# Column sums of the norms nearer to the products, squares on VectorE alone, six first tiles ahead of the second norm, and another order of the seven products

## The chip, the cores and the metric

The kernel runs on one core of one Trainium2 chip. The metric is the device time of one launch in microseconds (us); of several runs the median is taken. The engines are TensorE (PE in the profile, with its weight loads as PEld), VectorE (DVE), ScalarE (ACT), GpSimd (POOL) and SyncE (SP, which here issues the DMA transfers).

## The reference, cut to what matters

Two layers of a decoder with 1024 tokens and 1024 channels, in float32:

```
u = RMSNorm(h);  [rq|rk|rv|rg|dq|dk|dv] = u @ W_in        # 1024 x 3072
ret = silu(rg) * RMSNorm(retention(rq, rk, rv))            # 4 heads
dif = RMSNorm(differential_attention(dq, dk, dv))          # 4 heads
h = h + concat(ret, dif) @ W_out
u = RMSNorm(h)
h = h + (silu(u @ W_gate) * (u @ W_up)) @ W_down           # hidden width 2816
```

and a last RMSNorm. The change touches the norms and the feed-forward.

## The kernel before, in words

Channels lie on the partitions and tokens along the free axis, so `h` is eight tiles of 128x1024. A float32 factor is split in two parts, `hi` (a cast by ScalarE) and `lo` (the rest, a subtraction by VectorE or GpSimd), and each product takes three matmuls: hi by hi, hi by lo, lo by hi (`product`, lines 244 to 246; `mm3`, lines 268 to 270).

A norm works on one half of the tokens (512). `squares` lets ScalarE square the eight tiles of `h` and adds the squares up in one tile `acc`; VectorE does the adds, but those of k = 2 and 4 go to GpSimd. `rsqrt_rows` lets TensorE sum the columns of `acc` (line 378) into a few PSUM columns, a short chain of VectorE and ScalarE makes the inverse roots of them (lines 383 to 390), and after `gap` more units of TensorE's other work four transposes (line 394) spread the result over a bank. `yield lag` before it sets how many units of other work stand between the last square and the column sums; a unit is one matmul of 512 columns. The norm's generators are woven into the products of the output projection (`two_halves`) or of the feed-forward.

The feed-forward treats the tokens as two halves and the channels as two halves, and computes each 2x2 block product with seven products instead of eight. The right factors `b[0]` to `b[6]` come from the normed `h`: b[0] and b[1] need the first token half only (`seven_first`), the others the second half too (`seven_second`). Each of the 22 hidden tiles (`gate_up`; two weight tiles, one for gate and one for up) has seven products of 12 matmuls, numbered q = 0 to 6, into three PSUM banks `x`, `y` and `z`. Some banks are read between two products that add into them: after q = 2 ScalarE copies `x` (`u2`), after q = 3 ScalarE copies `z` (`z1`, line 951), and `c22` (line 963) is VectorE's read of `x` on the way. The order before is x y x z x z x. `first` (line 956) reads `y`, `second` (line 968) `z`, and `end` (line 973) `x`.

The left factors of a tile come from its two raw weight tiles, loaded by SP. `factors` plans their steps: `load`, `sums` (lines 903 to 905) and `last` (line 908) on VectorE, and five to seven `split`s. A split of product n is queued `LEAD` = 4 products ahead of it.

Since the second token half is normed only when TensorE is already in the feed-forward, q = 0 and 1 of the first `NPRE` = 5 tiles go ahead. Their `x` banks are kept until q = 2; the five `g0` results lie in `kb` and `acc` buffers. `seven_second` gives its steps to `Line.later`, which places them after a product with a given number. ScalarE, VectorE, GpSimd and SP have a written order in the feed-forward: each engine works its instructions off in the order of the code, and those that wait hold up those behind them. TensorE has a written order in the whole kernel.

In `down_fast` the same seven products run for two output tiles in turn (e = 0, 1), and each result is added to `h` (`add_h`, line 863). Its right factors (`right_factors`) come back from DRAM.

Of the kernel before, what the change touches and what calls it, by code (L numbers as in the profile page):

```python
# [27 lines left out]
NPRE = 5  # L28
# [3 lines left out]
TAGS7 = ["u", "u", "ka", "v", "sp", "u", "u"]  # L32
# [69 lines left out]
def shape_tables():  # L102
# [10 lines left out]
    kd = np.repeat(np.exp((P - 1 - c)[:, None] * lg[None, :]), 64, axis=1)  # L113
# [31 lines left out]
class Trunk:  # L145
# [29 lines left out]
    def consts(self):  # L175
# [5 lines left out]
        self.tabs = self.const("c_tabs", [P, 1026])  # L181
# [216 lines left out]
    def squares(self, h, sl, alone, pool, first=False):  # L398
        nc = self.nc
        tmp = (lambda: self.big("kb")[:, 0:512]) if first else self.tmp  # L400
        n = sl.stop - sl.start
        parts, acc = [], None
        for k in range(KT):
            s = (tmp() if k else self.t("acc", 1, [P, 512]))[:, :n]
            with nullcontext() if first else self.tc.high_priority():
                nc.scalar.activation(s, h[k][:, sl], AF.Square)
                if k >= KT - alone:
                    parts.append(s)
                elif acc is None:
                    acc = s  # L410
                    parts.append(s)
                else:
                    eng = nc.gpsimd if pool and k in (2, 4) else nc.vector
                    eng.tensor_tensor(out=acc, in0=acc, in1=s, op=ALU.add)
        return parts

    def norm_half(self, h, hf, gcol, us, pool=True, lag=14, first=False, keep=False):
        nc = self.nc
        sl = slice(hf * HT, hf * HT + HT)
        parts = self.squares(h, sl, 0, pool, first)  # L420
        yield lag
        y = yield from self.rsqrt_rows(parts, D)
# [14 lines left out]
    def seven_first(self, h, gcol, b, keep):  # L437

        nc = self.nc
        parts = self.squares(h, slice(0, HT), 0, True)  # L440
        yield 32
        y = yield from self.rsqrt_rows(parts, D)
# [6 lines left out]
    def seven_second(self, h, gcol, b, keep, line):  # L449
# [4 lines left out]
        parts = self.squares(h, sl, 0, True)  # L454
        yield 16
        y = yield from self.rsqrt_rows(parts, D, gap=9)
        own = self.t("u", 4, [P, KT, HT])
        b += [self.views(tag) for tag in TAGS7[2:4]]
# [3 lines left out]
        t2 = []  # L462
# [4 lines left out]

        def low(src, dst):
            v(out=dst[1], in0=src, in1=dst[0].bitcast(F32), op=ALU.subtract)

        def steps():
            b22 = self.views(TAGS7[5])
            for i in range(4):
                norm(t22[i], 4 + i)
                self.part(t22[i], b22[i], nc.gpsimd)
            yield
            for i in range(4):
                norm(t12[i], i)
            yield
            two = [self.big("sp") for _ in range(2)]  # L480
            t2.extend(two[i // 2][:, c[i % 2]] for i in range(4))
            for j in range(2):
                for i in (2 * j, 2 * j + 1):
                    v(out=b11[i], in0=t12[i], in1=b11[i], op=ALU.subtract)
                    v(out=t2[i], in0=t22[i], in1=b11[i], op=ALU.subtract)
                    nc.scalar.copy(b[2][i][0], t2[i])
                yield
            for i in range(4):
                low(t2[i], b[2][i])
                nc.scalar.copy(b[3][i][0], b11[i])  # L490
            yield
            for i in range(4):
                low(b11[i], b[3][i])
            yield
            for i in range(4):
                v(out=b21[i], in0=b21[i], in1=t2[i], op=ALU.subtract)
            yield
            b.append(self.views(TAGS7[4]))
            for i in range(4):
                v(out=b11[i], in0=t22[i], in1=t12[i], op=ALU.subtract)  # L500
                nc.scalar.copy(b[4][i][0], b11[i])
            yield
            b.append(b22)
            b.append(self.views(TAGS7[6]))
            for i in range(4):
                low(b11[i], b[4][i])
                nc.scalar.copy(b[6][i][0], b21[i])
            yield
            for i in range(4):
                low(b21[i], b[6][i])  # L510
            yield
        go = steps()
        for q in range(10):
            line.later(line.n + q, lambda: next(go))
# [259 lines left out]
    def ret_scores(self, x, n):  # L774
# [17 lines left out]
        if n < 7:  # L792
# [3 lines left out]
            nc.vector.tensor_tensor(out=kd, in0=tps[:, 0:256], in1=self.tabs[:, 768:1024], op=ALU.mult)  # L796
# [16 lines left out]
    def retention(self, l, x, mix):  # L813
# [3 lines left out]
        st = self.t("acc", 1, [P, 512])  # L817
# [5 lines left out]
        for n in range(8):  # L823
# [13 lines left out]
            if n < 7:  # L837
# [4 lines left out]
                for p in range(2):  # L842
                    for j in range(2):
# [3 lines left out]
                        nc.vector.scalar_tensor_tensor(out=sv, in0=sv, scalar=self.tabs[r, 1024 + p:1025 + p], in1=kv,  # L847
# [39 lines left out]
    def factors(self, line, at, pos, early=0, tags=("wr", "wr"), mixed=False):  # L887
# [8 lines left out]
        def split(n, i, k):  # L896
            src = s3[0] if i is None else r[i][:, c[k]]
            line.w[n] = self.wsplit(src, self.nc.vector if mixed and n % 3 == 0 else None)
# [21 lines left out]
        else:  # L920
            put(pos[2] - 4 - early, load, 0)
            put(pos[2] - 3 - early, load, 1)
            put(pos[2] - 1 - early, sums)
            put(pos[2] - 1 - early, last)
# [7 lines left out]
    def gate_up(self, line, at, b, pre, st, room, done, early=0):  # L932
# [4 lines left out]
        self.factors(line, at, {j: n0 + i for i, j in enumerate([range(7), range(2), range(2, 7)][pre])}, early)  # L937

        def go(name, tag, q):
            n = len(line.products)  # L940

            def run():
                if tag:
                    st[name] = self.bank(tag)
# [314 lines left out]
```

## Time and profile before

| | |
|---|---|
| median of 3 runs | 2340.5 us (2339.1 to 2342.1) |
| profiled execution | 2341.5 us, of which the span from first to last instruction is 2339.8 |
| TensorE busy | 2274.7 us, 97% of the span |
| VectorE, ScalarE, GpSimd busy | 1390.7 (59%), 1011.3 (43%), 850.9 (36%) us |
| DMA | 215.66 MB, mean 92 GB/s |
| granted TensorE clock | 0.988 of full speed |

The feed-forward of the first layer begins at 507.6 us of the span with the first product of tile 0. In a row of the profile `ps_mm<-u,w` means an output in a PSUM bank of tag mm made from tiles of tags u and w; numbers of buffers are left out. Times of single instructions are from the profiled execution.

### The profile page before, as it was taken

To read this page: it belongs to the slowest core of one execution; us is meant where nothing else is said; L and a number is where in the kernel's file an instruction comes from. 1 tells how busy PE (TensorE), PEld (TensorE's weight loads), DVE (VectorE), ACT (ScalarE), POOL (GpSimd) and SP (SyncE) were. 2 spreads that over 40 slices of the span, in tenths; PEclk is the share of its full clock that TensorE was granted. 3 is DMA by queue.
4 is the path that set the end of the run, shared out by engine and by line. 5 is a ranking of instruction groups with operands and counts; after the bars stand their busy time and mean duration, and the time that the engine had idled before them with its cause. 6 is when DMAs were issued, how large, how long until landed. Compare 5 with 4: busy or idle time off the path is not lost. (4 is left out here: it accounts for less than half of the span.)

```text
span 2339.8 us, 30724 instructions
## 1 busy us (share of the span) xinstructions
PE 2274.7 (97%) x11328; PEld 1906.9 (82%) x11328; DVE 1390.7 (59%) x2512; ACT 1011.3 (43%) x1905; POOL 850.9 (36%) x672
## 2 busy tenths in 40 slices
PE   7999999997999999999999999999889999999998
PEld 5888898876888888888888888988768888888887
DVE  7777603968543433896557774058874444449855
ACT  5666623434333333543246665244443333345332
POOL 4111212144545455335231112212544545544351
PEclk8999999999999999999999999999999999999999
DMA  4312121101332322753232122111123232345522
GB/s 159 81 46 64 46 91 45 55 28 56 125 126 77 126 86 92 242 164 115 73 90 55 49 70 81 56 36 54 46 94 128 77 126 77 104 145 184 185 63 73
DMA packets 73926, 215.66 MB, mean 92 GB/s; under 512 B 7984, under 2 KB 10032, under 8 KB 73776
## 3 DMA queue, kind: packets, MB, share of 16 engines
q1 hardware_dynamic: 73776, 213.70, 28.5%
q8 instruction: 89, 1.46, 0.3%
q14 instruction: 61, 0.50, 0.1%
HBM read 161.24 MB, written 44.04 MB: 88 GB/s over the span
## 5 line engine op out<-in xcount | busy, mean ns | idle before, releaser
L221 POOL TENSOR_TENSOR w<-wr,w 128x512 fp32r<-128x512 f32 x302 | 430.3, 1437 | 497.9 <-ACT w L220 466.3
L261 POOL TENSOR_TENSOR w<-wr,w 128x512 fp32r<-128x512 f32 x140 | 186.6, 1339 | 576.4 <-ACT w L260 547.5
L268 PE MATMUL ps_mm<-u,w 128*128 128x512 f32 (+1 forms) x735 | 296.6, 404 | 0.0
L270 PE MATMUL ps_mm<-u,w 128*128 128x512 f32 (+1 forms) x735 | 288.0, 392 | 0.0
L269 PE MATMUL ps_mm<-u,w 128*128 128x512 f32 (+1 forms) x735 | 287.8, 392 | 0.0
L220 ACT CAST w<-wr 128x512 fp32r<-128x512 f32 x320 | 193.2, 619 | 154.3 <-DVE wr L905 74.7
L244 PE MATMUL ps_mm<-u,w 128*128 128x512 f32 x448 | 175.6, 392 | 5.6 <-DVE t L963 5.6
L246 PE MATMUL ps_mm<-u,w 128*128 128x512 f32 x448 | 174.8, 390 | 0.0
L245 PE MATMUL ps_mm<-u,w 128*128 128x512 f32 x448 | 174.8, 390 | 0.0
L270 PEld LDWEIGHTS ps_mm<-u,w 128*128 128x128 f32 x735 | 138.4, 188 | 30.4
L951 ACT COPY t<-ps_mm 128x512 f32<-128x512 f32 x80 | 47.0, 588 | 258.6 <-PE ps_mm L246 258.6
L268 PEld LDWEIGHTS ps_mm<-u,w 128*128 128x128 f32 x735 | 138.8, 189 | 24.1
L269 PEld LDWEIGHTS ps_mm<-u,w 128*128 128x128 f32 x735 | 138.8, 189 | 23.3
L260 ACT CAST w<-wr 128x512 fp32r<-128x512 f32 x140 | 86.0, 619 | 128.8 <-PE ps_t L269 38.5
L305 PE MATMUL ps_mm<-w,u 128*128 128x256 f32 x448 | 127.1, 284 | 1.0 <-DVE u L431 1.0
L303 PE MATMUL ps_mm<-w,u 128*128 128x256 f32 x448 | 127.9, 285 | 0.0
L304 PE MATMUL ps_mm<-w,u 128*128 128x256 f32 x448 | 126.8, 283 | 0.0
L863 DVE TENSOR_TENSOR a<-a,ps_mm 128x512 f32<-128x512 f32 (+1 forms) x148 | 98.7, 667 | 45.7 <-PE ps_mm L270 27.5
L577 DVE CUSTOM_DVE_ANT_0 sp<-ps_s,wr 128x512 f32<-128x512 f32 (+2 forms) x192 | 103.2, 551 | 34.3 <-PE ps_s L575 33.1
L581 ACT ACTIVATE sp<-sp,m 128x256 f32<-128x256 f32 (+7 forms) x128 | 99.2, 775 | 53.4 <-DVE m L580 52.9
L244 PE MATMUL ps_t<-u,w 128*128 128x512 f32 x256 | 104.2, 407 | 18.5 <-DVE kb L956 18.5
L903 DVE TENSOR_TENSOR t<-wr,wr 128x512 f32<-128x512 f32 x48 | 35.4, 737 | 123.0 <-DMA wr<-wts 123.0
(364 smaller groups left out, 5959.8 us busy)
## 6 DMA issues: line engine op xcount, KB each, us to landing
wr<-wts SPq DMA_DIRECT2D x192, 512.0 KB, 3.7
mx<-s_fast SPq DMA_DIRECT2D x56, 512.0 KB, 5.2
s_fast<-mx SPq DMA_DIRECT2D x48, 512.0 KB, 4.3
kb<-ka SPq DMA_DIRECT2D x64, 128.0 KB, 2.3
s_rest<-mx SPq DMA_DIRECT2D x12, 512.0 KB, 2.9
kb<-wts SPq DMA_DIRECT2D x12, 512.0 KB, 5.4
mx<-s_rest SPq DMA_DIRECT2D x12, 512.0 KB, 3.3
a<-xT SPq DMA_DIRECT2D x16, 256.0 KB, 5.4
```

The source lines that it names most:

```text
L220: nc.scalar.copy(h, src)
L221: (eng or nc.gpsimd).tensor_tensor(out=o, in0=src, in1=h.bitcast(F32), op=ALU.subtract)
L244: mm(ps, lhsT=wh[:, c], rhs=bh, start=first and i == 0, stop=False, skip_group_check=True)
L245: mm(ps, lhsT=wh[:, c], rhs=bl, start=False, stop=False, skip_group_check=True)
L246: mm(ps, lhsT=wl[:, c], rhs=bh, start=False, stop=i == 3, skip_group_check=True)
L261: nc.gpsimd.tensor_tensor(out=o, in0=raw[:, cols], in1=h.bitcast(F32), op=ALU.subtract)
L268: mm(out, lhsT=lh, rhs=rh, start=first, stop=False)
L269: mm(out, lhsT=lh, rhs=rl, start=False, stop=False)
L270: mm(out, lhsT=ll, rhs=rh, start=False, stop=last)
L303: mm(o, lhsT=uh, rhs=wh, start=k == 0, stop=False)
L304: mm(o, lhsT=uh, rhs=wl, start=False, stop=False)
L305: mm(o, lhsT=ul, rhs=wh, start=False, stop=k == KT - 1)
```

## The change

The parts of the change, in the order of the diff:

- `NPRE` is 6 instead of 5. The sixth tile's `x` takes a bank of tag s. `hold` lets the `y` of tiles 4 and 5 share one bank, and the `z` of tiles 0 to 5 another. `acc` has two buffers instead of one; to make room, the `kd` table is stored with 4 columns instead of 256 and spread by the access pattern.
- `squares` adds on VectorE alone. The squares of `norm_half` lie in `kb` buffers.
- `lag` is 11 in all norms but the very first layer's second half and the last norm; `gap` is 9 but in the first layer's first norm and the last.
- `seven_second` gives out its steps singly, three per product and later four, in the order in which the products need their results. All splits of its factors are made by VectorE.
- `factors`: tile 0's two weight tiles are loaded ahead of the section into `sp` buffers, and its `sums` stand ahead of the norm. `own` names products whose split is on VectorE.
- The order of the seven products is x y x z z x x: those of q = 4 and 5 are swapped, with their left and right factors, in `gate_up` and in `down_fast`.

TensorE, inside a tile of the first layer's feed-forward (tile 13): ps_mm is the tile's bank `x`, ps_s its bank `z`; v, sp and u hold right factors, w the left ones. In brackets stands the engine whose semaphore is waited for. Before, the end of q = 3 and the beginning of q = 4:

```order
L246 MATMUL ps_s_6981<-v_5023,w_6914 128x512
L244 MATMUL ps_s_6981<-v_5024,w_6913 128x512
L245 MATMUL ps_s_6981<-v_5026,w_6913 128x512
L246 MATMUL ps_s_6981<-v_5024,w_6914 128x512
L244 MATMUL ps_s_6981<-v_5024,w_6913 128x512
L245 MATMUL ps_s_6981<-v_5026,w_6913 128x512
L246 MATMUL ps_s_6981<-v_5024,w_6914 128x512
L244 MATMUL ps_mm_6920<-sp_5228,w_6933 128x512 [waits Activation_49]
```

and after, at the same place:

```order
L246 MATMUL ps_s_6978<-v_5016,w_6912 128x512
L244 MATMUL ps_s_6978<-v_5017,w_6911 128x512
L245 MATMUL ps_s_6978<-v_5019,w_6911 128x512
L246 MATMUL ps_s_6978<-v_5017,w_6912 128x512
L244 MATMUL ps_s_6978<-v_5017,w_6911 128x512
L245 MATMUL ps_s_6978<-v_5019,w_6911 128x512
L246 MATMUL ps_s_6978<-v_5017,w_6912 128x512
L244 MATMUL ps_s_6978<-u_5020,w_6930 128x512 [waits Activation_49]
```

The product that follows q = 3 now adds into the same bank ps_s, and its first matmul waits for ScalarE, whose copy `z1` (`COPY t_1259_6995<-ps_s_6978`) reads that bank after q = 3. In the same way the last product, q = 6, now follows another one into ps_mm and waits for VectorE's `c22`.

VectorE in the same tile, before (t holds `u2`, `z1` and the sums' first result, wr the raw weights, mx the tile's results):

```order
L956 TENSOR_TENSOR mx_6958<-ps_t_6939,t_1250_6937 128x512
L903 TENSOR_TENSOR t_1264_7012<-wr_6956,wr_6976 128x512
L904 TENSOR_TENSOR wr_6976<-wr_6976 128x512
L905 TENSOR_TENSOR wr_6956<-wr_6976,wr_6956 128x512
L963 TENSOR_TENSOR t_1263_6998<-ps_mm_6920,t_1263_6998 128x512
L908 TENSOR_TENSOR wr_6956<-wr_6956 128x512
L968 TENSOR_TENSOR mx_6958<-ps_s_6981,t_1259_6978 128x512
L973 TENSOR_TENSOR mx_6958<-mx_6958,ps_mm_6920 128x512
```

and after:

```order
L936 TENSOR_TENSOR mx_6955<-ps_t_6936,t_1246_6934 128x512
L881 TENSOR_TENSOR t_1260_7009<-wr_6953,wr_6973 128x512
L882 TENSOR_TENSOR wr_6973<-wr_6973 128x512
L883 TENSOR_TENSOR wr_6953<-wr_6973,wr_6953 128x512
L948 TENSOR_TENSOR mx_6955<-ps_s_6978,t_1255_6975 128x512
L886 TENSOR_TENSOR wr_6953<-wr_6953 128x512
L943 TENSOR_TENSOR t_1259_6995<-ps_mm_6917,t_1259_6995 128x512
L953 TENSOR_TENSOR mx_6955<-mx_6955,ps_mm_6917 128x512
```

`c22` (line 963, now 943) and `second` (968, now 948) have changed places; ahead of `c22` stands `last` and no longer `sums`.

VectorE at the start of the first layer's feed-forward, right behind the inverse roots of the second token half, before (u is the normed half, kb the `g0` results, a the tiles of `h`):

```order
L956 TENSOR_TENSOR kb_4906<-ps_t_4976,t_901_4974 128x512
L465 SCALAR_TENSOR_TENSOR u_5018<-a_688_3898,c_gains,ps_s_5013 128x512
L465 SCALAR_TENSOR_TENSOR u_5018<-a_689_3899,c_gains,ps_s_5013 128x512
L465 SCALAR_TENSOR_TENSOR u_5018<-a_690_3900,c_gains,ps_s_5013 128x512
L465 SCALAR_TENSOR_TENSOR u_5018<-a_691_3901,c_gains,ps_s_5013 128x512
L903 TENSOR_TENSOR t_928_5074<-wr_4972,wr_5006 128x512
L904 TENSOR_TENSOR wr_5006<-wr_5006 128x512
L905 TENSOR_TENSOR wr_4972<-wr_5006,wr_4972 128x512
L908 TENSOR_TENSOR wr_4972<-wr_4972 128x512
L465 SCALAR_TENSOR_TENSOR u_5018<-a_684_3894,c_gains,ps_s_5013 128x512
```

and after:

```order
L221 TENSOR_TENSOR w_4984<-wr_4928,w_4983 128x512
L881 TENSOR_TENSOR t_905_4989<-sp_4930,sp_4932 128x512
L882 TENSOR_TENSOR sp_4932<-sp_4932 128x512
L883 TENSOR_TENSOR sp_4930<-sp_4932,sp_4930 128x512
L886 TENSOR_TENSOR sp_4930<-sp_4930 128x512
L465 SCALAR_TENSOR_TENSOR u_5011<-a_684_3894,c_gains,ps_s_5006 128x512
L465 SCALAR_TENSOR_TENSOR u_5011<-a_685_3895,c_gains,ps_s_5006 128x512
L465 SCALAR_TENSOR_TENSOR u_5011<-a_686_3896,c_gains,ps_s_5006 128x512
L936 TENSOR_TENSOR kb_4906<-ps_t_4996,t_906_4994 128x512
L221 TENSOR_TENSOR w_5048<-wr_4987,w_5047 128x512
L465 SCALAR_TENSOR_TENSOR u_5011<-a_687_3897,c_gains,ps_s_5006 128x512
```

Tile 0's `sums` have moved ahead of the norm, the read of `y` (956, now 936) comes after three steps of it, and splits of left factors (221) stand between.

The diff, cut:

```diff
-NPRE = 5
+NPRE = 6
-TAGS7 = ["u", "u", "ka", "v", "sp", "u", "u"]
+TAGS7 = ["u", "u", "ka", "v", "u", "u", "sp"]
...
-    def squares(self, h, sl, alone, pool, first=False):
+    def squares(self, h, sl, alone, kb=False, first=False):
...
-            s = (tmp() if k else self.t("acc", 1, [P, 512]))[:, :n]
+            s = (tmp() if k else self.t("acc", 2, [P, 512]))[:, :n]
...
-                    eng = nc.gpsimd if pool and k in (2, 4) else nc.vector
-                    eng.tensor_tensor(out=acc, in0=acc, in1=s, op=ALU.add)
+                    nc.vector.tensor_tensor(out=acc, in0=acc, in1=s, op=ALU.add)
...
-    def norm_half(self, h, hf, gcol, us, pool=True, lag=14, first=False, keep=False):
+    def norm_half(self, h, hf, gcol, us, lag=11, gap=9, first=False, keep=False):
...
     def seven_first(self, h, gcol, b, keep):
-        yield 32
-        y = yield from self.rsqrt_rows(parts, D)
+        yield 11
+        y = yield from self.rsqrt_rows(parts, D, gap=9)
...
     def seven_second(self, h, gcol, b, keep, line):
-        yield 16
+        yield 11
...
+        ops = [lambda i=i: norm(t12[i], i) for i in r]
+        ops += [lambda i=i: norm(t22[i], 4 + i) for i in r]
+        for i in r:
+            ops.append(lambda i=i: sub(b11[i], t12[i], b11[i]))
+            ops.append(lambda i=i: sub(t2[i], t22[i], b11[i], 2, i))
+        ops += [lambda i=i: low(t2[i], b[2][i]) for i in r]
+        ops += [lambda i=i: self.part(b11[i], b[3][i], nc.vector) for i in r]
+        ops += [lambda i=i: self.part(t22[i], b[4][i], nc.vector) for i in r]
+        ops += [lambda i=i: sub(b11[i], t22[i], t12[i]) for i in r]
+        ops += [lambda i=i: sub(b21[i], b21[i], t2[i]) for i in r]
+        for q, src in ((5, b11), (6, b21)):
+            ops.append(lambda q=q: b.append(self.views(TAGS7[q])))
+            ops += [lambda i=i, q=q, src=src: self.part(src[i], b[q][i], nc.vector) for i in r]
+        for i, op in enumerate(ops):
+            line.later(line.n + (i // 3 if i < 21 else 7 + (i - 21) // 4), op)
...
     def factors
-            put(pos[4], split, pos[4], None, 0)
-            put(pos[5], split, pos[5], 0, 1)
+            put(pos[4], split, pos[4], 0, 1)
+            put(pos[5], split, pos[5], None, 0)
...
     def gate_up
-            line.add(go("x", None, 4), c22)
-            line.add(go("z", None, 5), second)
+            line.add(go("z", None, 4), second)
+            line.add(go("x", None, 5), c22)
             line.add(go("x", None, 6), end)
...
     def feed_forward
-            st[t]["tag"] = ["mm", "mm", "mm", "o", "t"][t]
+            st[t]["tag"] = ["mm", "mm", "mm", "o", "t", "s"][t]
...
+            if t > 3:
+                st[t]["bank_y"] = hold
+            st[t]["bank_z"] = hold
...
+            kw = {"early": (-1, -1, 0), "tags": ("sp", "sp"), "own": range(2 * NPRE, 2 * NPRE + 5, 2)} if t == 0 else {}
...
     def down_fast
-                                                ("z", "s", 1, 1), ("x", None, 1, 1), ("z", None, 0, 1),
+                                                ("z", "s", 1, 1), ("z", None, 0, 1), ("x", None, 1, 1),
                                                 ("x", None, 1, 0))):
```

More of the change, by code (lines that the diff above doesn't have):

```diff
@@ L466, in norm, with sub @@
                                            in1=y, op0=ALU.mult, op1=ALU.mult)
+        def sub(out, x, z, q=None, i=0):
+            v(out=out, in0=x, in1=z, op=ALU.subtract)
+            if q is not None:
+                nc.scalar.copy(b[q][i][0], out)
         def low(src, dst):
             v(out=dst[1], in0=src, in1=dst[0].bitcast(F32), op=ALU.subtract)
[L471 to L511, printed above, removed]
@@ L512, in seven_second @@
-        go = steps()
-        for q in range(10):
-            line.later(line.n + q, lambda: next(go))
+        r = range(4)
+        ops = [lambda i=i: norm(t12[i], i) for i in r]
[5 more added lines that the diff above has]
+        ops += [lambda i=i: self.part(b11[i], b[3][i], nc.vector) for i in r]
@@ L920, in factors @@
         else:
[L921 to L924, printed above, removed]
+            n = pos[2] - LEAD
+            n0, n1, n2 = early or (n - 4, n - 3, n - 1)
+            line.later(n0, lambda: load(0))
+            line.later(n1, lambda: load(1))
+            line.later(n2, sums)
+            line.later(n2, last)
         if 2 in pos:
```

60 lines of the change are left out of this document (34 added, 26 removed).

## The prediction

> **What bounds the kernel now.** I read the page's busy shares first, then the table of stretches, then what TensorE waited for, then single rows at the places that the change touches.
>
> ```profile
> span 2339.8 us, 30724 instructions
> PE 2274.7 (97%) x11328; PEld 1906.9 (82%) x11328; DVE 1390.7 (59%) x2512; ACT 1011.3 (43%) x1905; POOL 850.9 (36%) x672
> ```
>
> TensorE is busy for 97% of the span, no other engine for more than 59%. The table of stretches shows where the rest lies. Its columns are the stretch, its length, and the busy time and instructions of PE, PEld, DVE, ACT and POOL, then the granted clock and the DMA.
>
> ```profile
> 507.00:572.00 65.00, 50.55 (x194) 39.99 (x193) 56.78 (x69) 29.60 (x54) 33.87 (x23) 0.87 0.16 49
> 572.00:970.00 398.00, 398.00 (x1749) 327.81 (x1748) 178.40 (x246) 150.09 (x268) 194.28 (x142) 1.00 0.34 115
> 1150.00:1200.00 50.00, 46.52 (x234) 39.39 (x233) 35.75 (x51) 22.38 (x42) 25.68 (x25) 0.93 0.40 137
> 1662.00:1726.00 64.00, 49.28 (x194) 38.55 (x193) 57.86 (x68) 29.45 (x53) 34.02 (x23) 0.89 0.17 50
> 1726.00:2125.00 399.00, 398.82 (x1751) 328.10 (x1750) 181.41 (x247) 149.94 (x268) 194.63 (x142) 1.00 0.35 116
> ```
>
> The two rows of 398 and 399 us are the gate and up products and the fast part of the down projection of each layer. TensorE never rests there: whatever makes it wait there adds to the time in full. The two rows of 64 and 65 us are the way into the feed-forward, where TensorE idles some 14.5 us per layer at a mean clock of 0.87 to 0.89; the row at 1150 is the norm between the layers. What TensorE waited for, over the whole span (total, times, longest), and in the stretch 1150:1200 (last row):
>
> ```profile
> PE ps_t L244 <- DVE kb L956: 18.5, 4, 5.1
> PE ps_s L378 <- DVE acc L414: 12.1, 6, 3.5
> PE ps_mm L244 <- DVE t L963: 5.6, 2, 2.8
> ...
> PE ps_s L378 <- DVE acc L414: 3.5, 1, 3.5
> ```
>
> So VectorE holds TensorE up on the way in: bank ps_t comes free only when L956 has read it, and L956 stands behind the norm's steps.
>
> **Part 1: products that write one bank twice in a row.** The diff swaps pos[4] and pos[5]. In each of the 22 tiles of a layer the second product into `z` now follows the first at once, and the last product into `x` follows the one before it at once. In between, ScalarE must copy `z` (`z1`, line 951) and VectorE must read `x` (`c22`, line 963). Before, a whole product of 12 matmuls, 2.72 us (398 us over 1749 matmuls is 0.227 each), lay over each of those reads, and the 398 us stretch shows that it hid them. Now nothing does. These rows price it: the last matmul of a `z` product and the next one, the copy behind it; the last matmul of an `x` product, the add behind it; and TensorE's restart at the one place where it already waited for that add.
>
> ```profile
> 657.15 0.39 PE L246 MATMUL ps_s<-v,w 128*128 128x512 f32 x1
> 657.38 0.40 PE L244 MATMUL ps_mm<-sp,w 128*128 128x512 f32 x1
> ...
> 657.63 0.59 ACT L951 COPY t<-ps_s 128x512 f32<-128x512 f32 x1 [1.15 <-PE ps_s L246]
> ...
> 640.81 0.39 PE L246 MATMUL ps_mm<-sp,w 128*128 128x512 f32 x1
> ...
> 641.31 0.69 DVE L963 TENSOR_TENSOR t<-ps_mm,t 128x512 f32<-128x512 f32 x1 [1.34 <-PE ps_mm L246]
> ...
> 569.02 0.68 DVE L963 TENSOR_TENSOR t<-ps_mm,t 128x512 f32<-128x512 f32 x1
> ...
> 569.75 0.50 PE L244 MATMUL ps_mm<-u,w 128*128 128x512 f32 x1 [2.80 <-DVE t L963]
> 570.09 0.39 PE L245 MATMUL ps_mm<-u,w 128*128 128x512 f32 x1
> ```
>
> A matmul follows the last after 0.23 us. The copy ends at 658.22, 1.07 after the start of the last `z` matmul. TensorE restarts 0.05 us after a reader ends (569.70 to 569.75), and its first step is 0.34 instead of 0.23. So the `z` wait costs 1.07 + 0.05 - 0.23 + 0.11 = 1.00 us. The add ends at 642.00, 1.19 after its matmul: 1.19 + 0.05 - 0.23 + 0.11 = 1.12 us. A tile pays 2.12 us, 44 tiles 93 us.
>
> The lower end: a reader that starts the instant the last matmul ends (0.39) and no slow restart, 0.39 + 0.59 - 0.23 = 0.75 and 0.39 + 0.69 - 0.23 = 0.85, so 70 us. The upper end: the adds of the trace did not all find VectorE free.
>
> ```profile
> DVE t L963 <- PE ps_mm L246: 37.5, 22, 4.2
> ```
>
> 22 adds waited for the product, of the 44 that there are; the rest stood behind other work, above all the three `sums` of the next tile. If half of the new adds came 0.9 us late, 20 us more, 113 in all. I stay with 93: in the new order `sums` stand ahead of `second`, a whole product before the add, and only the single `last` (L886) comes between. ScalarE has the same cast ahead of the copy as before.
>
> In the fast down projection the same swap leaves one product between (the two sets alternate), 2.72 us for an add of 0.69; I take 0, up to 3 us where `sums` lie ahead. What is queued behind the waiting matmuls is only TensorE's own stream; loads, casts and GpSimd's splits get more time, and nothing waits for them there.
>
> **Part 2: the way into the feed-forward.** Here VectorE sets the time. Before, its norm steps run from 520.70 to the add at 569.02; first row, the stretch; second, a stretch of it with GpSimd idle:
>
> ```profile
> 520.70:569.00 48.30, 36.68 (x141) 28.62 (x140) 47.35 (x52) 22.85 (x40) 26.21 (x16) 0.89 0.15 48
> 550.10:554.90 4.80, 4.65 (x11) 3.68 (x12) 4.80 (x9) 1.67 (x3) 0.00 (x0) 0.51 0.32 105
> ...
> 507.61 0.39 PE L244 MATMUL ps_mm<-u,w 128*128 128x512 f32 x1
> 513.93 0.34 PE L378 MATMUL ps_s<-c_ones,acc 128*128 128x1 f32 x1 [2.08 <-DVE acc L414]
> ...
> 515.80 0.16 DVE L383 TENSOR_SCALAR nx<-ps_s 128x4 f32<-128x4 f32 x1 [2.02 <-PE ps_s L378]
> ...
> 516.87 0.16 DVE L390 SCALAR_TENSOR_TENSOR ny<-nx,ny 128x4 f32<-128x4 f32 x1
> ...
> 520.70 0.75 DVE L465 SCALAR_TENSOR_TENSOR u<-a,c_gains,ps_s 128x512 f32<-128x512 f32 x1 [1.44 <-PE ps_s L394]
> ```
>
> Eight instructions start in the quiet 4.80 us, 0.60 each. 52 of them alone would be 31.2 us; the stretch took 17.1 more with 16 GpSimd instructions in it, so each of those costs VectorE 1.07 us. Before, the way in began at 507.61 (product 0) and the last product of tile 0 began at 569.75, 62.1 us later; its 14 products of 2.72 us and 1.4 us of sums and transposes are 39.5, so 22.6 us were lost.
>
> After: the same stretch, from the first L465 to the first `c22`, holds 61 VectorE instructions by the order (t22's low halves and the splits of products 6, 8, 10, 12, 14 and 16 come to VectorE) and about 7 of GpSimd: 61 x 0.60 + 7 x 1.07 = 44 us. It begins earlier. Squares no longer go through GpSimd and the column sums stand one product into the section, at 2.7 us; 9 matmuls and four transposes later it is 6.2; a split and tile 0's `sums`, now ahead of the norm, hold VectorE until about 8.3. The add then ends at 8.3 + 44 + 0.7 = 53.0 us. Without waits 16 products, 1.4 us and the 2.12 of part 1 are 47.0, so 6 us stay lost, mostly as waits for L936 of products 7 and 9 (the new number of L956) and for the last right factors. The gain is 22.6 - 6 = 16.6 us per layer, 33 in both. Ends: nothing lost, 45 us; VectorE as slow per instruction as before (61 x 0.93 = 57, lost 19), 7 us. I take 33, since the 1.07 comes from this stretch itself. Tile 0's two loads now go out before the section, into `sp`, ahead of three others in SP's queue; a load lands 3.7 us after its issue (next row), well before `sums` at 5 us and the splits that use the others, so I count 0.
>
> ```profile
> wr<-wts SPq DMA_DIRECT2D x192, 512.0 KB, 3.7
> ```
>
> **Part 3: the other norms.** Between the layers the 3.48 us wait for `acc` (L414, two of its adds on GpSimd) and the slower clock after it (granted 0.93 over 50 us) cost 3.5 us and, for some nine steps at 0.43 as in the rows below, 1.8, together 5.3. With all adds on VectorE the sum should be there on time; it is also asked for three matmuls, 0.7 us, earlier. I take a gain of 4.5, between 0 and 5.3. The first-half norms had no wait; they keep 9 or more matmuls over a chain of 1.2 us (515.80 to 517.03, L383 to L390) and cost 0, at most 1 each. The kernel's first norms keep their places in TensorE's order, the smaller `kd` table is a 128x256 operation as before, squares in `kb` use two buffers in turn: 0, plus or minus 1.
>
> **Sum.** The profiled execution took 2341.5 (span 2339.8). 2341.5 + 93 - 33 - 4.5 = 2397. It lay 1.0 above the median of the runs, 2340.5, so I predict 2396, slower by 2.4%.
>
> **The clock after a wait.** These rows show TensorE 3 us behind the idle of 2.08 at 513.93, behind one of 4.14 and behind one of 1.25:
>
> ```profile
> 517.05 0.63 PE L244 MATMUL ps_t<-u,w 128*128 128x512 f32 x1
> 517.48 0.63 PE L245 MATMUL ps_t<-u,w 128*128 128x512 f32 x1
> ...
> 540.52 0.50 PE L244 MATMUL ps_t<-u,w 128*128 128x512 f32 x1 [4.14 <-DVE kb L956]
> ...
> 541.45 0.63 PE L244 MATMUL ps_t<-u,w 128*128 128x512 f32 x1
> 541.88 0.63 PE L245 MATMUL ps_t<-u,w 128*128 128x512 f32 x1
> ...
> 130.50 0.52 PE L600 MATMUL ps_t<-c_ident,sp 128*128 128x128 f32 x3 [1.25 <-DVE sp L662]
> 130.77 0.48 PE L268 MATMUL ps_mm<-u,w 128*128 128x512 f32 x1
> 131.09 0.39 PE L269 MATMUL ps_mm<-u,w 128*128 128x512 f32 x1
> ```
>
> After the two long ones steps are 0.43, half speed; after the short one they are not. The new waits idle 0.7 to 0.9 us, so I add nothing. [...]
>
> **Rivals.**
> A. The waits are hidden after all, and the time falls: TensorE reaches the second `z` product only once the copy is done. For it: ScalarE and VectorE are less than half busy in the 398 us stretch. Against: the copy cannot start before the product ends, and no other matmul stands between. It decides at (33 + 4.5) / 88 = 0.43 us per wait; at no cost the time is 2303. Chance 0.04.
> B. Each wait, or each pair, brings the half clock, some nine steps of 0.43 instead of 0.23, 1.8 us: 44 to 88 times, 79 to 158 us, 2475 to 2554. For it: an idle of 2.08 us was enough. Against: the 1.25 above. Chance 0.06.
> C. The way in gains nothing, because VectorE, with 9 instructions more, is as late as before: 2396 + 33 = 2429. For it: VectorE was full there (56.78 of 65 us). Against: 16 GpSimd instructions become about 7. Chance 0.06.
> D. My forecast. With 80 to 110 for the waits and 50 to 25 for all gains together it is 2340.5 + 80 - 50 = 2370 to 2340.5 + 110 - 25 = 2425; the outer ends of both at once I leave out. Chance 0.80. The last 0.04 is for sums between these, around 2350.
>
> **How the numbers follow.** 2396 is D's. The range 2370 to 2425 is D's, and leaves out 0.20. A measurement of this kernel can tell about 0.2%, 4.7 us. Faster: A, 0.04. Same: 0.01, where a cheap wait just meets the gain. Slower: D, B, C and most of the rest, 0.95.
>
> **What would show it.** In the stretch of the gate and up products the waits of TensorE list L931 (the copy, on ScalarE) and L943 (the add) some 44 times each, at 0.7 to 1.0 us, with the granted clock still at 1.00, and a tile takes 21.2 us instead of 19.05. On the way in the waits for the ps_t bank shrink but stay; at 1180 there is no wait over 1 us. I am wrong if those two lines are missing or near 0.2 us, or if steps of 0.43 appear behind them.

## The result: slower by 3.1%, and the profile after

| | before | after | ratio (95% interval) |
|---|---|---|---|
| median of the runs | 2341.3 us (2339.1 to 2343.4, 4 runs) | 2414.8 us (2411.2 to 2416.4, 4 runs) | 1.0312 (1.0294 to 1.0330) |
| span of the profiled execution | 2339.8 us | 2414.6 us | |

The change costs 73.5 us; 55.5 were forecast, and the time lies in the range of 2370 to 2425. The page of the changed kernel, and its table of stretches (length, busy time and instructions of PE, PEld, DVE, ACT and POOL, then the granted clock and the DMA):

```profile
PE 2293.5 (95%) x11328; PEld 1896.0 (79%) x11328; DVE 1391.1 (58%) x2552; ACT 1008.7 (42%) x1905; POOL 784.6 (32%) x632
```

```profile
505.00:565.00 60.00, 53.39 (x223) 42.64 (x222) 52.62 (x76) 28.35 (x53) 19.75 (x12) 0.94 0.16 46
580.00:990.00 410.00, 379.52 (x1618) 300.25 (x1617) 163.97 (x227) 135.69 (x243) 172.24 (x131) 1.00 0.31 105
1190.00:1240.00 50.00, 46.31 (x245) 39.89 (x245) 34.40 (x52) 22.35 (x41) 25.39 (x23) 0.93 0.39 137
```

In the gate and up products (second row), where TensorE had been busy for all of 398 us, it now rests 30.5 us of 410, at a granted clock of 1.00. On the way in (first row) it rests 6.6 of 60 us instead of 14.5 of 65. The norm between the layers (third row) is as it was: 46.3 of 50 us busy, clock 0.93. What TensorE waited for, over the whole span (total, times, longest):

```profile
PE ps_s L244 <- ACT t L931: 35.2, 44, 2.9
PE ps_mm L244 <- DVE t L943: 31.0, 38, 1.4
PE ps_s L244 <- DVE a L841: 7.9, 6, 2.6
```

L931 (the copy of `z`) and L943 (`c22`) are there 44 and 38 times (six more `c22` waits, 5 us, stand under the banks ps_t, ps_o and ps_s, for tiles whose `x` lies there). L841 is the add of the down projection, a line that had no entry there before.

The start of each of the 210 products of a feed-forward can be read from both traces. What a stage took beyond 2.722 us for each of its products, both layers together, against the terms of the prediction:

| stage | before | after | difference | forecast |
|---|---|---|---|---|
| up to the first feed-forward | 507.6 | 505.2 | -2.4 | 0 |
| way in, to the end of tile 0 | 47.3 | 24.8 | -22.5 | -33 + 4.2 for two waits a layer |
| tiles 1 to 21 | 3.2 | 91.0 | +87.8 | +89 |
| fast down projection | 2.2 | 12.7 | +10.6 | 0 |
| between the feed-forwards | 556.3 | 556.6 | +0.3 | -4.5 |
| behind the second one | 79.9 | 81.0 | +1.1 | 0 |

The differences add up to 74.9, the spans differ by 74.8. The waits have the size that was forecast; the two gains are smaller, and the down projection is a loss that the forecast did not have.

One tile of the steady state, by the time of its instructions (start, length, engine, line; in brackets the idle before it and what ended that):

```profile
675.22 0.39 PE L246 MATMUL ps_s<-v,w 128*128 128x512 f32 x1
676.28 0.50 PE L244 MATMUL ps_s<-u,w 128*128 128x512 f32 x1 [0.68 <-ACT t L931]
676.62 0.39 PE L245 MATMUL ps_s<-u,w 128*128 128x512 f32 x1
...
681.63 0.39 PE L246 MATMUL ps_mm<-u,w 128*128 128x512 f32 x1
682.80 0.50 PE L244 MATMUL ps_mm<-sp,w 128*128 128x512 f32 x1 [0.79 <-DVE t L943]
683.14 0.39 PE L245 MATMUL ps_mm<-sp,w 128*128 128x512 f32 x1
...
675.64 0.59 ACT L931 COPY t<-ps_s 128x512 f32<-128x512 f32 x1 [1.09 <-PE ps_s L246]
...
682.06 0.69 DVE L943 TENSOR_TENSOR t<-ps_mm,t 128x512 f32<-128x512 f32 x1 [1.43 <-PE ps_mm L246]
```

Both readers had been idle before (1.09 and 1.43 us) and start 0.42 and 0.43 us after the start of the last matmul of their product. The step from 675.22 to 676.28 is 1.06 instead of 0.23, that from 681.63 to 682.80 is 1.17, and behind each one step of 0.34 follows; then TensorE is at 0.23 again. That is 0.95 + 1.05 = 2.0 us; from tile to tile it comes to 2.0 to 2.1.

### The profile page after: what moved, and what is told of

The parts are those of the page before. It is cut to its first block, busy times and chain, and to the rows that moved or that the text cites. A ratio compares the mean times of both kernels' runs of the same rounds, so it can differ in the third digit from the quotient of the medians.

```text
span 2414.6 us, 30677 instructions
## 1 busy us (share of the span) xinstructions
PE 2293.5 (95%) x11328; PEld 1896.0 (79%) x11328; DVE 1391.1 (58%) x2552; ACT 1008.7 (42%) x1905; POOL 784.6 (32%) x632
## 4 chain that ended last, share of the span: by engine, by line
PE 78%; DVE 12%; ACT 4%; issue 2%; DMA 2%; POOL 0%; DVEq 0%; SPq 0%; ACTq 0%; POOLq 0%
PE ps_mm L244 8%; PE ps_mm L246 7%; PE ps_mm L245 7%; PE ps_mm L268 6%; PE ps_mm L270 6%; PE ps_mm L269 6%; PE ps_s L244 5%; PE ps_s L246 4%; PE ps_s L245 4%; PE ps_mm L305 2%; PE ps_mm L303 2%; PE ps_mm L304 2%; PE ps_t L244 2%; PE ps_t L246 2%; PE ps_t L245 2%
## 5 line engine op out<-in xcount | busy, mean ns | idle before, releaser
L221 POOL TENSOR_TENSOR w<-wr,w 128x512 fp32r<-128x512 f32 x282 | 380.3, 1359 | 472.4 <-ACT w L220 468.4
L261 POOL TENSOR_TENSOR w<-wr,w 128x512 fp32r<-128x512 f32 x140 | 185.8, 1333 | 565.6 <-ACT w L260 539.2
L931 ACT COPY t<-ps_mm 128x512 f32<-128x512 f32 x76 | 44.7, 588 | 345.2 <-PE ps_mm L246 345.2
L244 PE MATMUL ps_mm<-u,w 128*128 128x512 f32 x432 | 168.5, 390 | 0.0
L246 PE MATMUL ps_mm<-u,w 128*128 128x512 f32 x432 | 168.4, 390 | 0.0
L245 PE MATMUL ps_mm<-u,w 128*128 128x512 f32 x432 | 168.2, 389 | 0.0
L221 POOL TENSOR_TENSOR w<-t,w 128x512 fp32r<-128x512 f32 x54 | 79.9, 1480 | 230.2 <-ACT w L220 230.2
L244 PE MATMUL ps_s<-u,w 128*128 128x512 f32 x256 | 107.9, 422 | 43.1 <-ACT t L931 35.2
L841 DVE TENSOR_TENSOR a<-a,ps_mm 128x512 f32<-128x512 f32 (+1 forms) x148 | 98.6, 667 | 48.5 <-PE ps_mm L246 35.0
```

The lines of the kernel that those rows point to most:

```text
L221: (eng or nc.gpsimd).tensor_tensor(out=o, in0=src, in1=h.bitcast(F32), op=ALU.subtract)
L244: mm(ps, lhsT=wh[:, c], rhs=bh, start=first and i == 0, stop=False, skip_group_check=True)
L245: mm(ps, lhsT=wh[:, c], rhs=bl, start=False, stop=False, skip_group_check=True)
L246: mm(ps, lhsT=wl[:, c], rhs=bh, start=False, stop=i == 3, skip_group_check=True)
L261: nc.gpsimd.tensor_tensor(out=o, in0=raw[:, cols], in1=h.bitcast(F32), op=ALU.subtract)
```

## Experiments

In these kernels a line or two were added near the top, so that the line numbers are higher by one to three: L245 is the product's first matmul, L379 the column sums, L414 the squares' add, L842 the add of the down projection. `ORD` is the old order in the new numbering.

**1. The old order back.** The version with all of it:

```diff
+ORD = (0, 1, 2, 3, 5, 4, 6)
 def gate_up
+        order = ORD if pre != 2 or at != self.ff_at else range(7)
-        self.factors(line, at, {j: n0 + i for i, j in enumerate([range(7), range(2), range(2, 7)][pre])}, **kw)
+        self.factors(line, at, {j: n0 + i for i, j in enumerate([order, order[:2], order[2:]][pre])}, **kw)
...
-            line.add(go("z", None, 4), second)
-            line.add(go("x", None, 5), c22)
+            two = {4: ("z", second), 5: ("x", c22)}
+            for q in order[4:6]:
+                line.add(go(two[q][0], None, q), two[q][1])
 def right_factors, down_fast
-        for q in range(7):
+        for p, q in enumerate(ORD):
```

> The changed kernel with the old order x y x z x z x of the seven products in the tiles 1 to 21 of each layer and in the fast down projection; tile 0 and everything else as changed. Theory (the swap costs what the trace of the changed kernel shows: 44.2 and 43.6 us in tiles 1 to 21 of the two layers, 6.5 and 4.1 us in the down projection, and the rest of the change is a gain): 2414.8 - 87.8 - 10.6 = 2316 us, below the kernel before. Rival 1 (the down projection's waits come from VectorE's splits there, not from the order): 2327 us. Rival 2 (the waits return at other places, because the six tiles ahead or the splits on VectorE cause them): above 2341 us.

> The same, but the down projection keeps the changed order (z after z, x after x). Theory: 2414.8 - 87.8 = 2327 us, with waits for L841's successor in the down projection of 6 to 10 us in all as in the changed kernel. If the order in the down projection costs nothing, this and the kernel with both undone give the same time.

Measured: 2319.7 us with both undone, ratio to the kernel before 0.9908 (0.9893 to 0.9922); 2332.2 us with the down projection left in the new order, 0.9960 (0.9945 to 0.9975). They lie 4 and 5 us above the 2316 and 2327 that were expected; no run here looks for these few us. The gate and up products of the first, a stretch of its table:

```profile
580.00:940.00 360.00, 360.00 (x1582) 296.63 (x1582) 158.43 (x213) 133.02 (x239) 179.16 (x130) 1.00 0.34 115
```

No rest is left there. So the swap is the whole of the loss: without it the change is a gain of some 20 us. The second kernel keeps this row among TensorE's waits, which the first does not have:

```profile
PE ps_s L245 <- DVE a L842: 10.2, 6, 3.0
```

Its down projections take 13.7 us beyond their products, those of the first 2.5; the medians differ by 12.5. Rival 1 falls too: VectorE has as many splits in both kernels, and only the one with the new order waits 10 us for the add.

**2. The swap alone, in the kernel before.**

```diff
+ORD = (0, 1, 2, 3, 5, 4, 6)
-        self.factors(line, at, {j: n0 + i for i, j in enumerate([range(7), range(2), range(2, 7)][pre])}, early)
+        self.factors(line, at, {j: n0 + i for i, j in enumerate([ORD, ORD[:2], ORD[2:]][pre])}, early)
-            line.add(go("x", None, 4), c22)
-            line.add(go("z", None, 5), second)
+            line.add(go("z", None, 5), second)
+            line.add(go("x", None, 4), c22)
```

> The kernel before with one edit: the products q = 4 and 5 of each hidden tile change places (x y x z z x x), in the gate and up products only. Theory (the price belongs to the order alone, 2.04 us a tile): 2341.3 + 42 x 2.04 = 2427 us, up to 4 more for the two tiles 0. Rival (the price needs the other parts of the change, such as the splits on VectorE): near 2341 us. A second rival (half of the adds stand behind the three sums of the next tile, 0.9 us late): 2447 us.

Measured: 2425.2 us, 1.0360 (1.0343 to 1.0378), 85 us more than the kernel before. Its waits (L952 is `z1`, L964 is `c22`):

```profile
PE ps_mm L245 <- DVE t L964: 33.4, 40, 1.7
PE ps_s L245 <- ACT t L952: 31.1, 44, 1.2
```

The tiles 1 to 21 of both layers take 87.1 us more than before, 2.07 a tile, and the way in 1.8 less. The price is that of the order, in either kernel: putting the order into the kernel before costs 85, taking it out of the changed kernel's gate and up products brings 83. The adds behind `sums` do not come late by the 20 us of the second rival, since in this order too `sums` stand ahead of `second`.

**3. How long a pause may be before the clock falls.**

```diff
-                nc.scalar.copy(st[to], st[name])
+                for _ in range(1 + more):
+                    nc.scalar.copy(st[to], st[name])
```

`more` is 0 but for `z1` of the tiles 7 to 18, where it is 1, 2, 3 and 4 for three tiles each.

> The changed kernel; in the tiles 7 to 18 of each layer ScalarE copies z one to four times more before the second z product may start (three tiles with each number), in the others as changed. The idle of TensorE before that product should be 0.8 us with no extra copy and then some 1.3, 1.85, 2.4 and 2.9. Theory P (a wait costs its length and one slow step): 60 extra copies x 0.53 = 32 us, 2447 us, no step of 0.43 behind any of the waits. Theory C (past an idle of about 2 us the clock halves for 1.8 us): the 12 tiles with three or four more pay 1.8 each besides, 2469 us, with steps of 0.43 behind those waits and none behind 0.8 and 1.3.

Measured: 2466.3 us (one run). In the rows L246 to L248 are a product's matmuls and L934 the copy. Waits of 1.29 us (one more copy) and of 1.91 us (two more), and the stretches behind three waits:

```profile
677.03 0.50 PE L246 MATMUL ps_s<-u,w 128*128 128x512 f32 x1 [1.29 <-ACT t L934]
677.37 0.39 PE L247 MATMUL ps_s<-u,w 128*128 128x512 f32 x1
...
742.96 0.50 PE L246 MATMUL ps_s<-u,w 128*128 128x512 f32 x1 [1.91 <-ACT t L934]
743.29 0.39 PE L247 MATMUL ps_s<-u,w 128*128 128x512 f32 x1
...
744.56 0.63 PE L246 MATMUL ps_s<-u,w 128*128 128x512 f32 x1
744.98 0.63 PE L247 MATMUL ps_s<-u,w 128*128 128x512 f32 x1
```

```profile
742.96:744.20 1.24, 1.24 (x5) 1.04 (x6) 1.14 (x2) 0.46 (x1) 0.70 (x1) 1.00 0.00 0
744.20:747.60 3.40, 3.40 (x10) 2.60 (x9) 1.39 (x2) 0.62 (x1) 1.88 (x2) 0.52 0.00 0
...
864.64:868.05 3.41, 3.40 (x15) 2.83 (x16) 0.35 (x1) 0.99 (x2) 2.54 (x2) 1.00 0.00 0
...
840.22:843.20 2.98, 2.98 (x7) 2.40 (x8) 0.41 (x1) 1.06 (x2) 2.44 (x2) 0.50 0.03 5
```

All six waits of 1.29 us are followed by steps of 0.34, then 0.23. Behind the 1.91 us the first steps are fast as well; 1.24 us later the clock is at half for 3.4 us and each step is 0.43. So it went six times out of six. Of the longer waits some did nothing: one of 2.52 us ended at 840.22 with the half clock behind it, the next of the same length at 864.64 without. Twelve of the 18 waits of 1.9 us and more cost 1.3 to 1.6 us besides their length. The time is that of theory C, but not by its rule: there it should have been the 12 with three or four copies.

**4. The same length each time.** As in the kernel of the last experiment, with `more` = 3 in the tiles 4 to 20.

> The changed kernel with three extra copies of z before the second z product in the tiles 4 to 20 of each layer: 34 waits of the same length, an idle of some 2.5 us each. In the run with one to four extra copies, waits of this length had steps of 0.43 behind them in four cases and none in two, and the places where the clock fell lay on a grid of 3.41 us. Theory G (the clock is set for each window of 3.41 us by the idle in the window before; it halves where that idle is over some 1.75 us): whether a wait costs 1.6 us more depends on where in the grid it falls; 72% of places do ((3.41 - 2.53 + 2 x 0.78) / 3.41), some 24 of 34 waits, in runs of neighbouring tiles, since a tile of 23 to 24.6 us is near seven windows: 2414.8 + 102 x 0.58 + 24 x 1.6 = 2512 us. Rival I (each wait past an idle of about 2 us brings the half clock, and the two exceptions had another cause): all 34, 2528 us. Rival N: the length of the wait alone counts from the second such wait on: 2475 us.

Measured: 2507.1 us (one run). Two neighbouring waits of the same length:

```profile
687.62 0.80 PE L246 MATMUL ps_s<-u,w 128*128 128x512 f32 x1 [2.53 <-ACT t L934]
688.22 0.63 PE L247 MATMUL ps_s<-u,w 128*128 128x512 f32 x1
...
712.14 0.50 PE L246 MATMUL ps_s<-u,w 128*128 128x512 f32 x1 [2.53 <-ACT t L934]
712.48 0.39 PE L247 MATMUL ps_s<-u,w 128*128 128x512 f32 x1
```

Of the 34 waits 20 had the half clock behind them (24 by theory G, 34 by I, none by N), 14 had not; a tile takes some 24.6 us with the half clock and 23.0 without, so that the wait moves on, and the two kinds mostly alternate. So the length of a wait alone, 2.53 us in both of these rows, did not decide here; its place did, as G says. Where the places lie is read from the granted clock of the same trace. Here are two stretches at half clock with the one between them, and then two windows of 3.41 us, each with the window that follows it (the granted clock is the third number from the end):

```profile
1858.16:1861.57 3.41, 3.41 (x9) 2.65 (x9) 0.00 (x0) 0.25 (x1) 2.38 (x2) 0.50 0.98 326
1861.57:1923.01 61.44, 51.41 (x219) 40.48 (x219) 19.34 (x29) 22.97 (x41) 21.61 (x17) 1.00 0.22 75
1923.01:1926.42 3.41, 3.41 (x9) 2.67 (x8) 0.00 (x0) 0.66 (x2) 2.52 (x2) 0.50 0.00 0
...
803.44:806.85 3.41, 1.44 (x7) 0.86 (x5) 0.81 (x2) 2.22 (x5) 1.28 (x1) 1.00 0.67 256
806.85:810.26 3.41, 2.86 (x7) 2.28 (x8) 1.27 (x2) 1.64 (x3) 2.31 (x2) 0.50 0.00 0
922.90:926.31 3.41, 1.48 (x7) 0.90 (x5) 0.69 (x1) 2.22 (x5) 1.28 (x1) 1.00 0.00 0
926.31:929.72 3.41, 2.82 (x12) 2.36 (x13) 0.00 (x0) 1.58 (x3) 2.27 (x2) 1.00 0.02 5
```

The two falls lie 64.85 us apart, 19 times 3.413; in the traces of the kernel before and of the changed one the stretches at one clock are whole multiples of 3.413 us too (from 556.31 to 1006.87 in the changed one 450.56 us, 132 times 3.413), but for the last one, at the end of the trace. At 803.44 TensorE was idle for 1.97 us of the window (3.41 - 1.44) and the next window is at half clock; at 922.90 it was idle for 1.93 and the next one is not. Over the tiles 1 to 21 of this run and of the one before it, all 26 windows with 1.97 us of idle or more were followed by the half clock, and none with less than 1.91; between the two, six were (at 1.91) and three were not. The ends of matmuls are modelled in the trace, so that the border is no sharper than that. So in these tiles G fits with some 1.9 us in place of its 1.75, which was the author's estimate and which no run shows; its sum then gives (3.41 - 2.53 + 2 x 0.6) / 3.41 = 61%, 21 of 34 waits instead of 24. That is the border of these tiles alone: in the kernel before, TensorE was idle for 1.35 us of the window from 1667.54, where the column sums stand, and the next one is at half clock.

**5. The norm between the layers.** The version with the old order, and:

```diff
-                       ... self.norm_half(h, 1, 8, nus),
+                       ... self.norm_half(h, 1, 8, nus, 32),
```

> The changed kernel with the old order as in both_back, and one number more: the second half's norm between the layers asks for its column sums 32 units after the last square instead of 11. Theory (the wait of 3.6 us there ends with the last add of squares, which stands behind the last tile of h and has nothing to do with GpSimd's former share; 21 units of 0.227 us more work ahead of it cover it): the wait goes, and with it the slower clock after it, 3.6 + 1.6 = 5 us, 2319.7 - 5 = 2314.5 us. Rival (the work behind the norm is late instead, because u of the second half comes 4.8 us later): 2320 us or more.

Measured: 2312.6 us, 0.9881 (0.9867 to 0.9895), the fastest of all, 26.7 us below the kernel before in the same runs (2339.2). The stretch of that norm, in the version with the old order alone, and then here, with the first of the column sums here:

```profile
1150.00:1200.00 50.00, 46.36 (x251) 39.98 (x250) 31.82 (x53) 21.65 (x43) 24.56 (x22) 0.97 0.36 118
```

```profile
1150.00:1200.00 50.00, 50.00 (x291) 44.07 (x291) 36.43 (x71) 26.01 (x53) 25.20 (x24) 1.00 0.43 133
```

```profile
1167.21 0.61 PE L379 MATMUL ps_s<-c_ones,acc 128*128 128x1 f32 x5
```

No idle stands ahead of the sums any more, and between the two feed-forwards 5.8 us less pass (556.5 to 550.7). The lag set the wait, and nothing behind the norm was late for it.

**6. Two parts of the change undone, one at a time,** in the version with the old order: seven splits back to GpSimd (the `own` arguments left out of `feed_forward`), and two adds of squares back to GpSimd:

```diff
-                    nc.vector.tensor_tensor(out=acc, in0=acc, in1=s, op=ALU.add)
+                    eng = nc.gpsimd if pool and k in (2, 4) else nc.vector
+                    eng.tensor_tensor(out=acc, in0=acc, in1=s, op=ALU.add)
```

> As in both_back, but the seven splits of left factors that the change gave to VectorE on the way into each feed-forward go to GpSimd, as all others do. Theory (VectorE sets the time there, an instruction costs it 0.60 us, and each GpSimd instruction beside it costs it 1.07 us): VectorE gets 7 x 0.60 = 4.2 us less and 7 x 1.07 = 7.5 us more, 3.3 us a layer, 2319.7 + 6.6 = 2326 us. Rival (GpSimd's instructions cost VectorE little, so that VectorE is relieved): 2319.7 - 8.4 = 2311 us.

> As in both_back, but two of the eight squares (k = 2 and 4) of the norms between and inside the layers are added by GpSimd again, as in the kernel before; lags as changed. Theory: the column sums at the way into the feed-forward come late again by some 2 us (before: a wait of 2.08), with the slower clock after it 2 to 3.7 us a layer if VectorE's steps behind it move by as much; the norm between the layers, whose wait ends with the last add of VectorE, stays at 3.6 us: 2319.7 + 4 to 7 = 2324 to 2327 us. Rival (the eight adds are not what the column sums waited for, and the lag alone decides): 2320 us.

Measured: with the splits back, 2321.0 us, 0.9918 (0.9905 to 0.9932), not told apart from 0.9908 (0.9893 to 0.9922). VectorE's stretch from the first norm step to tile 0's `c22` has 56 instructions instead of 62 and 13 or 14 of GpSimd instead of 8 or 9, and is as long as before (46.4 and 45.6 us, against 46.8 and 46.1). Six VectorE instructions are paid with about five of GpSimd: a GpSimd instruction costs VectorE an estimated 0.7 us here (6 x 0.60 / 5), neither 1.07 nor nothing. The stretch begins 1.3 us later than with the splits on VectorE (10.9 us behind the first product instead of 9.6), and each way in loses 0.8 to 0.9 us more, which the times of the runs do not tell apart.

With the squares back: 2325.7 us, 0.9937 (0.9922 to 0.9951), 6 us more, as the theory said for the whole:

```profile
PE ps_s L379 <- DVE acc L415: 12.3, 6, 4.9
```

The column sums at the two ways in wait 2.3 us again (0.1 with VectorE alone), and each way in loses 3.2 to 3.5 us more. One part of the theory is wrong: the wait between the layers did not stay, it grew from 3.6 to 4.9.

## Why the prediction came out right, and what was off by 19 us

**Part 1, the waits in the tiles: right in place, price and count.** 2.12 us a tile were forecast from the copy's end, the restart and one slow step; the tiles 1 to 21 took 2.09 more each (87.8 / 42). The choice of 93 rather than 113 held because in this order `c22` found VectorE idle, as the row at 682.06 shows; 40 of the 42 waits for it in these tiles have 0.78 to 0.85 us. Rival A, hidden waits, fell with the first table: a wait cost 1.0 us, and A needed less than 0.43.

**The clock: right.** It stood at 1.00 over the 410 us. Rival B, the half clock behind each wait or each pair, is not borne out at these lengths: the 84 pauses of the tiles 1 to 21, of 0.68 to 0.85 us but for three of 1.2 to 1.4, and the six of 1.29 in experiment 3 left no half-speed step. That fits experiment 4: the two pauses of a tile lie 6.5 us apart (676.28 and 682.80), so that no window of 3.41 us holds both; the window with the most idle in these tiles, from 2163.99, has 1.38 us. The margin is not large, though: pauses of 1.91 us brought the half clock six times of six.

**Part 1, the fast down projection: the step that failed.** It set 2.72 us of cover against an add of 0.69 and took 0, up to 3. It came to 10.6. The add did not find VectorE free:

```profile
999.76 1.78 DVE L236 TENSOR_TENSOR u<-mx,u 128x512 fp32r<-128x512 f32 x1
1001.46 1.77 DVE L221 TENSOR_TENSOR w<-wr,w 128x512 fp32r<-128x512 f32 x1
1003.16 0.67 DVE L841 TENSOR_TENSOR a<-a,ps_mm 128x512 f32<-128x512 f32 x1
...
1006.16 0.67 DVE L841 TENSOR_TENSOR a<-a,ps_s 128x512 f32<-128x512 f32 x1
```

```profile
1006.98 0.76 PE L244 MATMUL ps_s<-u,w 128*128 128x512 f32 x1 [2.57 <-DVE a L841]
```

The bank that the matmul at 1006.98 writes was read by the add at 1006.16, which stood in VectorE's order behind splits of right and left factors (two of them 1.8 us long, beside GpSimd) and two other adds. The prediction had counted the add's own length and not what is queued ahead of it. That the waits come with the order is shown by experiment 1; that the queue makes the add late is read from this trace, and no run moves the splits. The waits stand where the first right factors come in, and again in the last group.

**Part 2, the way in: right in kind, the gain too large.** Forecast -33, measured -22.5 - 4.2 = -26.7. The stretch was to begin 8.3 us behind the first product and to take 44.7 up to the end of `c22`, at 53.0:

```profile
511.83 1.67 DVE L882 TENSOR_TENSOR sp<-sp 128x512 f32<-128x512 f32 x1
...
514.87 0.74 DVE L465 SCALAR_TENSOR_TENSOR u<-a,c_gains,ps_s 128x512 f32<-128x512 f32 x1
```

```profile
560.24 0.69 DVE L943 TENSOR_TENSOR t<-ps_mm,t 128x512 f32<-128x512 f32 x1 [0.77 <-PE ps_mm L246]
```

It began at 9.6 (514.87 - 505.25), since one of the steps ahead took 1.67 beside a GpSimd split where 0.60 had been counted, and took 46.1, with the 61 instructions that were counted ahead of `c22` and 8 of GpSimd instead of 7. `c22` ended at 55.7, in the second layer too. That is 2.7 us a layer of the 6.3 that both lost more than forecast; the kernel before also loses 1.1 us less on its second way in than on the first, from which the forecast took both. Experiment 6 shows that the price of 1.07 for a GpSimd instruction is not a constant; with the eight of this stretch and `c22` the sum by it still fits (62 x 0.60 + 8 x 1.07 = 45.8).

In part that fit is luck, because VectorE did not set the end of the stretch alone: `c22` waited 0.77 us for TensorE. TensorE was late there by tile 0's own wait for `z1`:

```profile
549.61 0.39 PE L246 MATMUL ps_s<-v,w 128*128 128x512 f32 x1
552.87 0.80 PE L244 MATMUL ps_s<-u,w 128*128 128x512 f32 x1 [2.87 <-ACT t L931]
...
550.68 1.65 ACT L235 CAST sp<-mx 128x512 fp32r<-128x512 f32 x3
552.24 0.57 ACT L931 COPY t<-ps_s 128x512 f32<-128x512 f32 x1
```

In the later tiles the copy starts 0.42 us behind the last matmul's start, here 2.63, behind three casts of right factors in ScalarE's order; the wait is 2.87 us instead of 0.7 (2.83 in the second layer), and the clock is at half from 552.90 for 3.41 us. The prediction's "the same cast ahead of the copy as before" holds for the tiles 1 to 21 and not for tile 0. No run here gives tile 0 of the changed kernel the old order. The waits at the bank ps_t shrank as forecast, from 18.5 us in four places to 7.1 in three.

**Part 3, the norm between the layers: wrong.** Forecast -4.5, measured +0.3, and "at 1180 there is no wait over 1 us" was false: the wait, now at 1216, is 3.69 instead of 3.48.

```profile
1213.30 0.67 DVE L841 TENSOR_TENSOR a<-a,ps_mm 128x512 f32<-128x512 f32 x1
1214.07 0.63 ACT L406 ACTIVATE kb<-a 128x512 f32<-128x512 f32 x1 [1.81 <-DVE a L841]
1214.73 1.54 DVE L413 TENSOR_TENSOR acc<-acc,kb 128x512 f32<-128x512 f32 x1 [0.76 <-ACT kb L406]
...
1216.41 0.77 PE L378 MATMUL ps_s<-c_ones,acc 128*128 128x1 f32 x3 [3.69 <-DVE acc L413]
```

The step that failed put the wait down to the two adds on GpSimd. It ends with a chain behind the last tile of `h`: add, square, add, 3.1 us from 1213.30 to 1216.41, whoever adds the squares before. The two adds did count for 1.2 us (3.64 against 4.85 with them, at a lag of 11), but the lag went from 14 to 11 units in the same change and asked for the sums 0.7 us earlier. The prediction had seen that shift and had not priced it against a chain that starts with the last product. A lag of 32 takes the wait away.

**The small terms.** 2.4 us less ahead of the first feed-forward are no part of the change: with the kernel before and the swap alone, whose code ahead of it is the same, it began at 504.5, in the kernel before at 507.6. The sum of the misses in the traces is -1 for the tiles, +6.3 for the way in, +10.6, +4.8, -2.4 and +1.1, 19 us, which is the difference between the 2397 that the sum gave for the profiled execution and the 2416.4 that it took. Range D, which let the gains fall to 25 and the waits rise to 110, covers it, in part by luck: the room for dearer waits was meant for late adds in the tiles, which did not come, and took in the 10.6 us of the down projection, for which at most 3 had been set. Rival C, no gain on the way in, is refused by the table.

## What to carry to other kernels

Between two products into one bank that something must read in between, leave at least one product into another bank: the price without it was here the reader's whole latency with its restart, 0.95 and 1.05 us for the two places of a tile, although both readers had been idle before. When cover is counted for such a read, count what stands ahead of the reader in its engine's order, not the reader's own length. And before a wait is put down to a slow helper, follow the chain back from its last link: a lag moved by 21 units was worth 7 us here, a faster helper only what its own adds took, 1.2 us of that wait.

## What the runs showed of the hardware that was not expected

Whether a pause of TensorE brought the half clock depended in the experiments 3 and 4 on where it fell and not only on its length: 1.29 us never did (6 times), 1.91 us did 6 times of 6, 2.5 us did 4 times of 6 in one run and 20 of 34 in the other, 3.1 us twice of 6. By the granted clock it is the idle inside one window of 3.41 us that tells the cases of their tiles 1 to 21 apart: all 26 windows with 1.97 us and more had the half clock in the next window, none with less than 1.91 had. That 1.91 us did so each time is, by the author's estimate, a matter of place: these tiles take 24.0 us, near seven windows (23.9), so that three neighbouring waits all fell whole into a window. Where the clock fell, some 3.4 us at 0.43 per step followed (1.4 to 1.7 us lost, the slow first step among them), and they began 1.2 us behind the restart or within the pause (a first step of 0.60 instead of 0.34). There 1.91 us of idle in a window, 56% of its 3.41, was enough.
